# Eight-by-eight max pool subtracted from its own input: five buffers of five rows, smaller first pieces and a longer jump

## Chip, core, metric

One core of one Trainium2 chip. The metric is device time in microseconds (us) of the whole program, here of one core. The verdict for a change is faster, same or slower at a limit of 2%.

## The reference

```python
def reference(x):                       # x: 8 x 64 x 256 x 256, float32
    x_r = x.reshape(B, C, oH, 8, oW, 8)
    pooled = x_r.max(axis=(3, 5))
    upsampled = np.repeat(np.repeat(pooled, 8, axis=2), 8, axis=3)
    return (x - upsampled).astype(np.float32)
```

A "row" below is eight image lines, 2048 floats or 8 KB. Each of the 128 partitions holds whole rows and gets 128 of them: 134.22 MB come in, as many go out.

## The kernel before

```python
HEAD = [[2, 2]]      # the first tile, in pieces of so many rows
SIZE = 4             # rows of a whole tile
ROUNDS = 5           # turns of the vector engine's loop
TAIL = [2, 1, 1]     # the last tile, stored in pieces
SLOTS = 6            # buffers
SKIP = 52            # instructions that a jump passes
# ... (layout and semaphores cut)
    def pool_and_subtract(slot, lo, R, wait):
        # ...
        if wait is not None:
            take(wait, 16)                    # wait for the load
        nc.vector.tensor_reduce(...)          # max of each 8 x 8 window, R rows
        take(reduced, 1)
        for r in range(R):
            sub = nc.vector.tensor_tensor(...)  # in place, a row each
        sub.then_inc(ready, 1)
# ... SyncE: a load per piece; waits for stored[slot] before a buffer is loaded again
# ... ScalarE: a store per piece, after ready; at the end it waits for the last stores
        with nc.vector.If_eq(turns, 0):       # never taken: turns is ROUNDS
            for _ in range(SKIP):
                nc.vector.sem_inc(skipped, 1)
        # ... head pieces
        with nc.vector.Fori(0, ROUNDS):
            for j in range(SLOTS):
                slot = (HEADS + j) % SLOTS
                pool_and_subtract(slot, 0, SIZE, loaded[slot])
        # ... tail pieces
```

Three streams run side by side: loads, the vector engine, stores (vector engine and data queues are busy for 90% and 99.6% of the span, below). The guarded instructions never run (the page counts 364 instructions with a jump of 52 and, in jump_only, of 72); they move the loop to another place in the vector engine's instruction stream.

## Time and profile before

| | before |
|---|---|
| timed, median | 627.71 us |
| span of the profiled execution | 626.0 us |
| vector engine busy | 562.6 us (90%) |
| the two data queues, share of 16 DMA engines | 99.6% |

The page and its views are shown in the prediction. It is the last microseconds in slices of one microsecond; the columns are the slice, its length, busy time of the vector engine and of GpSimd, the TensorE clock, the mean busy share of the 16 DMA engines, and their rate in GB/s:

```profile
622.00:623.00 1.00, 0.00 (x0) 0.00 (x0) 1.00 0.95 401
623.00:624.00 1.00, 0.00 (x0) 0.00 (x0) 1.00 0.55 229
624.00:625.00 1.00, 0.00 (x0) 0.00 (x0) 1.00 0.02 8
```

A share of 0.06 is one DMA engine of sixteen (1/16). After 624 us one engine alone is still at work, for a part of the slice.

### The profile page before, as it was taken

What the parts mean: (1) busy time and instruction counts of PE and PEld (TensorE: products, weight loads), DVE (VectorE), ACT (ScalarE), POOL (GpSimd) and SP (SyncE); (2) the same over time, 40 slices, a digit from 0 to 9 for tenths busy, and PEclk for the clock granted to TensorE, in tenths of its full rate; (3) what the DMA queues carried; (4) which work ended last, traced back from release to release, by engine and by line L of the source; (5) the groups of instructions that cost most, each with busy time, mean ns of one, the idle gap of its engine ahead of it and who ended that gap; (6) DMA issues with size and microseconds to landing.
All of it is one profiled execution on the core that took longest, in us unless ns stands there. A gap on an engine that the chain in (4) does not pass through costs nothing. (4 is left out here: it accounts for less than half of the span.)

```text
span 626.0 us, 364 instructions
## 1 busy us (share of the span) xinstructions
DVE 562.6 (90%) x163; POOL 0.2 (0%) x4
## 2 busy tenths in 40 slices
DVE  4999999998998888988889888898888998888983
POOL 0000000000000000000000000000000000000000
DMA  8999999999999999999999999999999999999998
GB/s 369 399 436 437 436 436 436 436 433 427 429 431 436 427 431 436 436 436 436 436 436 436 436 431 429 427 433 429 431 433 436 436 436 436 436 436 436 436 429 343
DMA packets 9793, 268.45 MB, mean 429 GB/s; under 512 B 1088, under 2 KB 1088, under 8 KB 1088
## 3 DMA queue, kind: packets, MB, share of 16 engines
q1 hardware_dynamic: 4752, 134.22, 49.9%
q10 hardware_dynamic: 5040, 134.22, 49.7%
q14 instruction: 1, 0.01, 0.0%
HBM read 134.22 MB, written 134.22 MB: 429 GB/s over the span
## 5 line engine op out<-in xcount | busy, mean ns | idle before, releaser
L73 DVE TENSOR_REDUCE tops<-dat 128x128 f32<-128x8192 f32 (+2 forms) x35 | 278.3, 7953 | 48.9 <-DVEq L65 48.9
L85 DVE TENSOR_TENSOR dat<-dat,tops 128x2048 f32<-128x2048 f32 x128 | 285.0, 2286 | 5.2
L157 POOL MEMSET const-bfloat16-1.0<- 128x1 bf16 x1 | 0.1, 101 | 0.0
L157 POOL MEMSET const-uint8-127<- 128x1 uint8 x1 | 0.1, 101 | 0.0
L157 POOL MEMSET const-float32-0.0<- 128x1 f32 x1 | 0.1, 98 | 0.2 <-issue 0.2
L157 POOL MEMSET const-float32-1.0<- 128x1 f32 x1 | 0.1, 98 | 0.0
## 6 DMA issues: line engine op xcount, KB each, us to landing
dat<-in_x_dram SPq DMA_DIRECT2D x31, 4096.0 KB, 62.5
out_dram<-dat ACTq DMA_DIRECT2D x30, 4096.0 KB, 35.8
out_dram<-dat ACTq DMA_DIRECT2D x3, 2048.0 KB, 19.6
dat<-in_x_dram SPq DMA_DIRECT2D x2, 2048.0 KB, 9.6
out_dram<-dat ACTq DMA_DIRECT2D x2, 1024.0 KB, 9.3
```

The lines of the kernel that those rows point to most:

```text
L73: nc.vector.tensor_reduce(out=maxs if R > 1 else maxs[:, 0], in_=(wins.rearrange("p r ph ow pw -> p r ow ph pw") if R > 1 else wins[:, 0]. ...
L85: sub = nc.vector.tensor_tensor(out=wins[:, r], in0=wins[:, r], in1=maxs[:, r].unsqueeze(1).unsqueeze(3).to_broadcast([P, pH, oW, pW]), op ...
L157: nc = _bacc.Bacc("TRN2", target_bir_lowering=False, num_devices=1)
```

## The change

Fewer and larger transfers (tiles of five rows in five buffers), a head of small pieces so that the first result can be stored sooner, and a longer jump, meant to spare the loop a fetch of instructions in each turn.

```diff
-HEAD = [[2, 2]]
-SIZE = 4
-ROUNDS = 5
+HEAD = [[1, 1, 2], [2, 3], [5], [5], [5]]
+SIZE = 5
+ROUNDS = 4
 TAIL = [2, 1, 1]
-SLOTS = 6
-SKIP = 52
+SLOTS = 5
+SKIP = 72
@@
-                pool_and_subtract(i, lo, R, first[k])
+                pool_and_subtract(i % SLOTS, lo, R, first[k])
```

## The prediction

The sum in it is 0.36 us saved, from 627.71 to about 627.35. All of it comes from the steady transfers, per DMA engine 0.29 us for 64 packets fewer and 0.07 us for 8 completion writes fewer; every other part is put at 0. In rival (a), "a sixth of the bandwidth" is an estimate from the bytes of the two queues from 26 to 50 us, 7.18 against 3.41 MB with packets of 32 against 16 KB.

> **What bounds the kernel now.** I read first the page's busy shares, slices and waits, then the sums by stretch, then the transfers in order of time at both ends. The page:
>
> ```profile
> span 626.0 us, 364 instructions
> DVE 562.6 (90%) x163; POOL 0.2 (0%) x4
> GB/s 369 399 436 437 436 436 436 436 433 427 429 431 436 427 431 436 436 436 436 436 436 436 436 431 429 427 433 429 431 433 436 436 436 436 436 436 436 436 429 343
> q1 hardware_dynamic: 4752, 134.22, 49.9%
> q10 hardware_dynamic: 5040, 134.22, 49.7%
> q14 instruction: 1, 0.01, 0.0%
> ```
>
> The vector engine is 90% busy, but the two data queues together hold the 16 DMA engines for 99.6% of the span. Only the first two slices and the last fall well below 436 GB/s; the dips to 427 in the middle are whole packets falling into one slice or the next. The sums by stretch:
>
> ```profile
> 2.00:4.00 2.00, 0.00 (x0) 0.00 (x0) 1.00 0.88 295
> 18.00:26.00 8.00, 7.85 (x3) 0.00 (x0) 1.00 0.95 356
> 26.00:100.00 74.00, 73.41 (x22) 0.00 (x0) 1.00 1.01 436
> 100.00:580.00 480.00, 437.44 (x126) 0.00 (x0) 1.00 1.00 433
> 620.00:624.00 4.00, 0.00 (x0) 0.00 (x0) 1.00 0.89 375
> ```
>
> The last number is the rate. 433 holds both while the vector engine has no pause (26 to 100 us) and while it pauses before each tile (100 to 580 us), so its speed does not set the rate. Waits from 150 to 580 us:
>
> ```profile
> DVE tops L73 <- DVEq L65: 37.5, 23, 1.6
> ```
>
> It waits 1.6 us for each tile's load. And the end, in order of time:
>
> ```profile
> 598.35 4.42 DVE L73 TENSOR_REDUCE tops<-dat 128x64 f32<-128x4096 f32 x1 [1.64 <-DVEq L65]
> 614.39 2.29 DVE L85 TENSOR_TENSOR dat<-dat,tops 128x2048 f32<-128x2048 f32 x1
> ```
>
> The last subtract ends at 616.7 us, but that 1 MB store lands at 624.9: older stores were still queued. The end is bound by transfers too, and a vector engine that finished sooner would gain nothing.
>
> [...] from 26 to 50 us, while the loads run in 32 KB packets and the first stores in 16 KB ones, the queues moved 7.18 and 3.41 MB, 2 to 1; later, with 32 KB on both sides, 104.11 and 103.84. [...] The trace's instruction packets are 8 KB[...], and one falls in the span.
>
> **The change part by part.** Work is the same 128 rows of 8 KB per partition, each moved in and out.
>
> Steady transfers. A packet of 8, 16 or 32 KB occupies a DMA engine 309, 611 or 1213 ns, that is 301 ns per 8 KB and 9 ns more; successive packets start about 4 ns before the last has ended, so a packet really costs about 4.5 ns beyond its bytes at 27.2 GB/s (435.2 GB/s for 16). Check: a 4-row tile is 8 packets in and 8 out per DMA engine, 16 x (1204.7 + 4.5) ns, and two completion writes of 9 ns: 19.37 us; loads land every 19.36 us (114.15, 133.52, 152.88). With 5 rows: 16 x (1505.9 + 4.5) ns + 18 ns = 24.18 us, or 4.837 us a row against 4.841. Counted over the kernel: before 33 loads and 35 stores, 68 x 8 = 544 packets per DMA engine; after 29 loads (eight head pieces, 20, 1) and 31 stores (8, 20, 3), 480. Saved: 64 x 4.5 ns = 0.29 us and 8 x 9 ns = 0.07 us, 0.36 us together.
>
> Vector work. A reduce takes 2279, 4417, 8685 ns for 1, 2, 4 rows: 2135 per row and 144 fixed, so 6.55 us for 3 and 10.82 us for 5. Before 30 x 8.685 + 3 x 4.417 + 2 x 2.279 = 278.4 us; after 23 x 10.82 + 6.55 + 3 x 4.417 + 4 x 2.279 = 277.8 us. The 128 subtracts (2.205 us start to start) stay. A 5-row tile takes 10.82 + 5 x 2.205 + 0.13 = 22.0 us, under the 24.18 us of its transfers. 0.6 us less busy, on an engine that has slack: worth 0.
>
> Head. The first piece of one row should land about 2.4 us sooner (5.9 us in place of 8.3), and the first store be issued at about 10.6 in place of 17.5. But the DMA engines are already full of loads by then (441 GB/s from 4 to 18 us), and the same 24 rows of loads are issued at once in both kernels. Starting sooner moves bytes from load time to store time; it removes none. Worth 0, save for the one-time bubble where the first store joins the loads: 18 to 26 us at 356 GB/s loses about 1 us beside the plateau. It should move to about 13 us and stay about as long.
>
> Tail. Same pieces, same last store, and again stores are queued behind each other: worth 0.
>
> Slots. 25 rows of buffer in place of 24 (203 KB per partition by shapes in place of 195). A buffer's round of load, compute and store before is 62.5 + 17.9 + 35.8 = 116.2 us = 6 x 19.36. After it must be 5 x 24.18 = 120.9 us, of which compute 22; so 99 us of transfers, 4.1 tile transfers waiting or moving at any time. The DMA engines run dry only if both queues empty together[...].
>
> Jump. [...] Worth 0 as long as no fetch recurs each turn; even then a turn has 5 x 2.2 = 11 us of slack.
>
> Sum: 0.36 us saved, from 627.71 to about 627.35.
>
> **The rivals.** (a) Small store packets are starved. An 8 KB store packet against a 40 KB load packet gets a sixth of the bandwidth, so tile 0's stores drag. I followed it by hand: 8 rounds of row 0 against 16 and 24 KB loads end at about 22.6 us, 8 of row 1 at 34, 8 of two rows against 40 KB (2.125 us a round) at 51; slot 0 is free then, as before (its next load was issued at 51.7). Tile 1 frees at about 88 us, when some 3 rows of loads are still queued: close, but not dry, and the store backlog would take all the bandwidth anyway. So worth 0 in time; what it does is leave a deeper store queue and a shallower load queue than before. If both did run dry for some us: 628 to 632. (b) The vector engine becomes the bound, by a fetch each turn or by slots that come free late: against it stand 22.0 against 24.18 us per tile and the deep store queue; it needs over 10 us a turn lost. Then 630 to 645. (c) The earlier start counts in full because the early vector engine is never idle (the slices read 9 from the second on): then 2 to 5 us less, 623 to 625. The 8 us of queued stores behind the last subtract speak against it. (d) 40 KB packets run less well than 32 KB [...]: the 8, 16 and 32 KB sizes all lie on one straight line, which speaks against it; 1% worse would be 633.
>
> **Range and chances.** The three runs before differ by 0.35 us. The bubble and the ragged end may each move by some tenths. I predict 627.3, with 626.5 to 628.3 to hold 8 times in 10, a bit more room above for (a). Faster by 2% would mean under 615.2 us, and 268.44 MB at 435.2 GB/s take 616.8 alone: 0.005. Slower by over 2% needs (b) or (d) badly: 0.015. Within 2%: 0.98.
>
> **What would show it.** Right: both queues with 99% or more of the span; 40 KB packets and 4176 and 4464 packets on the two queues; loads landing 24.2 us apart; DVE busy about 562 us, 5-row reduces of 10.82 us, a wait of about 2.1 us before each in the second half; first store issued near 10.6 us and yet the same end; loads taking less time to land than 62.5 us and stores more than 35.8. Wrong: a slice in the middle well under 430 GB/s, an idle vector engine between 30 and 100 us, more than a few instruction packets, or a last store that lands 3 us after its issue (then the vector engine bounds the tail).

## The result

629.01 us in the median of six runs (628.81 to 629.48) against 627.71 (627.41 to 627.85): ratio 1.0023, 95% interval 1.0010 to 1.0036. By the limit of 2% that is "same", but it is a real 1.3 us the wrong way, and outside the predicted 626.5 to 628.3. A ratio here is the mean time of one kernel's fast runs over that of the other's of the same rounds, so not quite the ratio of the medians. All of these runs are fast.

The page of the changed kernel:

```profile
span 627.0 us, 342 instructions
DVE 561.3 (90%) x159; POOL 0.2 (0%) x4
q1 hardware_dynamic: 4176, 134.22, 49.8%
q10 hardware_dynamic: 4464, 134.22, 49.6%
q14 instruction: 1, 0.01, 0.0%
dat<-in_x_dram SPq DMA_DIRECT2D x23, 5120.0 KB, 41.7
out_dram<-dat ACTq DMA_DIRECT2D x23, 5120.0 KB, 57.0
```

The packet counts, the busy time of the vector engine and the shallower load queue (41.7 us from issue to landing) beside a deeper store queue (57.0) are as predicted. The sums by stretch:

```profile
12.00:18.00 6.00, 5.85 (x3) 0.00 (x0) 1.00 0.98 385
18.00:40.00 22.00, 21.71 (x7) 0.00 (x0) 1.00 1.01 433
40.00:46.00 6.00, 5.85 (x4) 0.00 (x0) 1.00 1.03 414
100.00:580.00 480.00, 442.40 (x122) 0.00 (x0) 1.00 1.00 433
580.00:620.00 40.00, 27.10 (x12) 0.00 (x0) 1.00 1.00 431
```

The plateau is the same 433 GB/s, and nothing runs dry. The bubble where stores join the loads has come in two halves, at 12 to 18 and at 40 to 46 us. The waits from 150 to 580 us:

```profile
DVE tops L73 <- DVEq L65: 34.5, 16, 2.7
```

That is 2.2 us before each tile, as predicted. The vector engine's end:

```profile
589.22 4.41 DVE L73 TENSOR_REDUCE tops<-dat 128x64 f32<-128x4096 f32 x1
605.25 2.29 DVE L85 TENSOR_TENSOR dat<-dat,tops 128x2048 f32<-128x2048 f32 x1
```

The last subtract ends at 607.5 us, 9.2 us sooner than before (616.7), and it gains nothing. Now the last slices, to be laid beside those of before:

```profile
622.00:623.00 1.00, 0.00 (x0) 0.00 (x0) 1.00 0.89 377
623.00:624.00 1.00, 0.00 (x0) 0.00 (x0) 1.00 0.10 41
624.00:625.00 1.00, 0.00 (x0) 0.00 (x0) 1.00 0.06 25
625.00:626.00 1.00, 0.00 (x0) 0.00 (x0) 1.00 0.02 8
```

Here the loss is. From 623 to 624 the share is 0.10 where it was 0.55: nearly all DMA engines have finished half a microsecond sooner than before. But from 624 to 625 it is 0.06, exactly one engine, busy all the time, and it goes on to 625.5.

The trace has a record for each packet with its start and duration, and a completion write of 4 bytes for each DMA engine at the end of each transfer. The 16 completion writes of the very last store tell how far apart the engines are (ns from the median engine, which stands first in us; worked out from these records):

```
before   median 623.63 us:  -209 -197 -182 -172 -171  -89  -19   -8    8   41   73   74  136  143  164   942
changed  median 623.05 us:  -164 -135 -116 -112  -39  -31  -25   -1    1   26   97  108  114  123  515  2454
```

In the changed kernel the median engine ends 0.58 us sooner than in before, but one engine is 2.45 us behind it where the late one of before was 0.94 behind. The load queue's 4176 packets are 29 loads of 144, eight data packets and a completion write for each of 16 engines. This fits with no engine taking over another's packets, and an engine that is late stays late: in the run before_long_jump below, the last completion writes of loads and stores alike stay 1.46 to 1.47 us behind the median from 50 us to the end. The kernel ends with its slowest engine.

The ledger of the two profiled executions (629.17 and 627.78 us, 1.39 apart): the median engine ends 0.58 sooner; the slowest is 1.51 further behind it; from its last packet to the span's end, 0.04 more; and the time outside the span (timed less span) is 2.20 against 1.78, 0.42 more. The sum is 1.39.

Where does the late engine lose its time? One packet in the span belongs to queue q14, which the trace calls an instruction packet: that it brings a part of the vector engine's program is read from the runs below, where its time moves with the jump (4.1 us with a jump of 72, 12.3 with 52). The records don't name the DMA engine of a packet; packets are followed by their times, as one starts about 4 ns before the last one of its engine ends. Packets at 4 us in the changed kernel and at 17 us in before, from the records:

```
            start ns  duration  queue         bytes
changed         4144       311  instruction    8192
                4451       841  load           8192   (309 is usual)
before         17261       309  instruction    8192
               17566      1795  load          32768   (1213 is usual)
```

The one instruction packet occupies an engine for 0.31 us and the load packet after it is stretched by 0.53 or 0.58 us: 0.84 and 0.89 us in all. In before that is nearly the whole lateness of 0.94. In the changed kernel it is 0.84 of 2.45 (the first load's completion writes already show one engine 838 ns late); 0.4 us more come by 19 us, while the stores join. The rest: six load packets after 50 us are stretched by more than 25 ns (in before, none), four of them, at 160.44, 209.26, 233.62 and 257.86 us, by 430, 164, 52 and 591 ns. The late engine's completion writes of the loads jump by 0.42, 0.17, 0.06 and 0.60 us at just these tiles. They lie one or two tile periods (24.18 us) apart, each within 0.4 us of the end of a store on the median engine (160.75, 209.14, 233.33, 257.54 us).

### The profile page after: what moved, and what is told of

It reads as the page before. It is cut to its first block, busy times and chain, and to the rows that moved or that the text cites. A ratio compares the mean times of both kernels' runs of the same rounds, so it can differ in the third digit from the quotient of the medians.

```text
span 627.0 us, 342 instructions
## 1 busy us (share of the span) xinstructions
DVE 561.3 (90%) x159; POOL 0.2 (0%) x4
## 3 DMA queue, kind: packets, MB, share of 16 engines
q1 hardware_dynamic: 4176, 134.22, 49.8%
## 5 line engine op out<-in xcount | busy, mean ns | idle before, releaser
L73 DVE TENSOR_REDUCE tops<-dat 128x160 f32<-128x10240 f32 (+3 forms) x31 | 277.7, 8958 | 41.7 <-DVEq L65 41.7
## 6 DMA issues: line engine op xcount, KB each, us to landing
dat<-in_x_dram SPq DMA_DIRECT2D x23, 5120.0 KB, 41.7
```

Source lines behind the costliest of these rows:

```text
L73: nc.vector.tensor_reduce(out=maxs if R > 1 else maxs[:, 0], in_=(wins.rearrange("p r ph ow pw -> p r ow ph pw") if R > 1 else wins[:, 0]. ...
```

## The experiments

The theory after the first look: the end is set by the slowest DMA engine; an instruction packet makes one engine late, and something else makes it later. "Late" below means behind the median engine. The rivals for that something: the longer jump by itself, the small head pieces, or five rows (40 KB packets, shallow load queue).

For each run the trace gave: the time of its instruction packet; the lateness of the slowest engine at the last store; the number of load and store packets between 50 and 600 us stretched by more than 25 ns; and the **gap**: on the median engine, the time from the end of a load to the end of the next store, in turns of one load and one store packet (2.42 us with 32 KB, 3.02 with 40 KB). That an engine takes them in turn is read from the records: in before from 100 to 580 us, a packet and the next of its engine are of different queues in all 2416 cases in which their times leave only one choice. The gap stays the same to within 0.1 turn from about 100 to 560 us, but for two runs that have a range in the table. It came to matter in the second round.

| run | timed median, lowest to highest | ratio to before | timed less span | instruction packet at us | gap | slowest late by us | stretched |
|---|---|---|---|---|---|---|---|
| before | 627.71, 627.41–627.85 | 1 | 1.78 | 17.3 | 6.9 | 0.94 | 0 |
| changed kernel | 629.01, 628.81–629.48 | 1.0023 | 2.17 | 4.1 | 3.0 | 2.45 | 6 |
| jump_only | 627.82, 627.71–630.33 | 1.0006 | 1.83 | 4.8 | 7.0 | 3.65 | 45 |
| head_only | 642.81, 642.21–644.31 | 1.0240 | 1.78 | 18.3 | 1.0–1.4 | 4.16 | 617 |
| five_rows_old_head | 628.78, 627.25–629.62 | 1.0010 | 2.25 | 4.7 | 6.0 | 2.69 | 15 |
| after_short_jump | 626.65, 626.42–626.77 | 0.9979 | 1.77 | 12.3 | 2.0 | 0.59 | 3 |
| before_delayed | 630.30, 629.63–633.11 | 1.0054 | 1.81 | 19.6 | 0.0–0.2 | 3.24 | 114 |
| head_only_delayed | 627.28, 626.87–627.79 | 0.9993 | 1.80 | 19.9 | 3.0 | 1.00 | 3 |
| short_jump_delayed | 626.72, 626.49–626.91 | 0.9985 | 1.79 | 12.9 | 4.0 | 0.30 | 2 |
| after_delayed | 627.41, 627.30–628.20 | 0.9998 | 2.23 | 4.1 | 5.0 | 1.24 | 2 |
| short_jump_gap3 | 626.65, 626.49–628.90 | 0.9995 | 1.79 | 12.3 | 3.0 | 0.30 | 0 |
| after_gap4 | 627.97, 627.44–632.99 | 1.0020 | 2.22 | 4.1 | 4.5 | 0.92 | 0 |
| before_later_fetch | 627.61, 627.34–627.77 | 0.9998 | 1.74 | 26.8 | 6.6 | 0.79 | 0 |
| before_long_jump | 630.07, 628.15–632.62 | 1.0049 | 2.02 | 4.5 | 7.0 | 1.46 | 0 |
| after_jump60 | 628.84, 628.64–628.94 | 1.0016 | 1.74 | 4.0 | 3.0 | 2.71 | 17 |

The columns from "timed less span" on are of the one profiled execution, with its span rounded to 0.1 us. All runs in the table are fast by the 1.5% rule, those near 633 us too. Before, run beside them, gave medians of 627.65 to 627.69.

### Round one: one part of the change at a time

**jump_only.**

```diff
-SKIP = 52
+SKIP = 72
```

> Before with nothing changed but the jump (72 in place of 52). Straggler theory (one DMA engine, held up by an 8 KB instruction packet, ends last; the rest of its lateness in the changed kernel comes from elsewhere): one instruction packet in the span, moved from 17 us to about 4, one DMA engine about 0.85 us behind the median at the end, time within 0.2 us of before (627.7). Rival, the jump itself costs the 1.3 us (by its early instruction packet): 628.7 to 629.3, lateness over 2 us.

Four of six runs gave 627.71 to 627.83, as the theory has it; two gave 630.05 and 630.33, and the profile fell on the latter: three engines over 3.5 us late, with store packets stretched from 58 to 95 us. The jump alone does not cost the steady 1.3 us; but the early instruction packet seems to make such single bad runs likelier. Before itself had one run of 629.07 among eleven in this round, so the kernel is not free of them.

**head_only.**

```diff
-HEAD = [[2, 2]]
+HEAD = [[1, 1, 2]]
-SKIP = 52
+SKIP = 49
```

> Before with the head's first tile cut into 1, 1, 2 rows, jump shortened by three so that the loop stands at the same instruction. Straggler theory: 627.6 to 627.9, one DMA engine about 0.9 us late, no stretched packets after 60 us. Rival, the small head pieces unsettle the DMA engines: 628.5 to 629.3, with stretched packets and lateness over 1.5 us.

Both expectations fell: 642.81 us, ratio 1.0240 (1.0227 to 1.0254), fifteen microseconds for one more head piece. The trace shows the DMA engines busy all the time and slow. From 130.5 to 134.5 us:

```profile
130.50:134.50 4.00, 4.00 (x2) 0.00 (x0) 1.00 1.06 377
100.00:580.00 480.00, 427.88 (x122) 0.00 (x0) 1.00 1.00 423
```

The first line is one burst, 377 GB/s; the second says that the plateau as a whole is at 423 in place of 433. The stretched load packets (525, three in four of them by 100 to over 1000 ns) come in bursts once a tile, where the engines pass from one store to the next, and only here is a load's end just one turn ahead of it. That gave the gap as a suspect.

**five_rows_old_head.**

```diff
-HEAD = [[1, 1, 2], [2, 3], [5], [5], [5]]
+HEAD = [[2, 2], [5], [5], [5], [5]]
-SKIP = 72
+SKIP = 78
```

> The changed kernel with the old head pieces of 2 and 2 rows and then four whole tiles of five (jump set so that the loop stands where it does in the changed kernel). If the small pieces cause the lateness: 627.0 to 627.4, since the median DMA engine should end near 623.1 us and the late one 0.9 later. If five slots or 40 KB packets cause it: 628.6 to 629.5, with stretched load packets after 60 us.

Scattered, 627.25 to 629.62, a median of 628.78. Neither expectation covers the scatter. The small pieces are not what makes the changed kernel slow: without them an early packet (4.7 us) and a late engine (2.69) are still there. And at a gap of six, 15 packets are stretched all the same. The load packets at 80.77 and 105.30 us are so by 334 and 391 ns, and at the completion of just these two loads the slowest engine has fallen behind by 414 ns more each time.

**after_short_jump.**

```diff
-SKIP = 72
+SKIP = 52
```

> The changed kernel with the old jump of 52. If the jump's place of the fetch causes the lateness: about 627.3, or more instruction packets and a time of 630 or more if [...] each turn fetches (each packet about 0.85 us on some DMA engine[...]). If the jump is not the cause and no turn fetches: 629.0 as the changed kernel.

626.65 us (626.42 to 626.77), ratio to before 0.9979, interval 0.9966 to 0.9992. Twenty instructions fewer in the jump turn the changed kernel's loss into a gain, and the time is below either expectation. The loop does not fetch in each turn: there is one instruction packet in the span, at 12.3 us. Its last slices:

```profile
622.00:623.00 1.00, 0.00 (x0) 0.00 (x0) 1.00 0.80 336
623.00:624.00 1.00, 0.00 (x0) 0.00 (x0) 1.00 0.04 16
624.00:625.00 1.00, 0.00 (x0) 0.00 (x0) 1.00 0.00 0
```

Nobody works after 624 us. The median engine ends at 622.94 us, as in the changed kernel (623.05), and the slowest 0.59 later. But two things changed at once: the packet came at another time, and as the first piece landed sooner (all engines by 5.08 us in place of 5.90) the first store came sooner and the gap is two instead of three. Round two separates them.

### Round two: moving the gap

A reduce with no use, ahead of the first real one, delays the first store and so shifts stores against loads (see the gaps in the table); everything else stays. The edit (with the jump one shorter, so that the loop keeps its place):

```diff
+                if k == 0:
+                    take(first[0], 16)
+                    nc.vector.tensor_reduce(out=idle[:, :], in_=dats[0][:, :DELAY],
+                                            axis=mybir.AxisListType.X, op=mybir.AluOpType.max)
-                pool_and_subtract(i, lo, R, first[k])
+                pool_and_subtract(i, lo, R, first[k] if k else None)
```

**before_delayed** (before, DELAY = 2048).

> Before with one idle reduce of one row (2.28 us) ahead of the first real one, so that the first store joins the loads two 32 KB load packets later. Boundary theory (what stretches load packets is how many packets lie between the end of one load and the end of the next store on a DMA engine; bad at one, as in the kernel with only the head changed): the gap goes from seven packets to one, and the time to 638 to 645 with hundreds of stretched packets. Rival, small pieces or early stores in themselves did it: 627.5 to 628.5, no stretched packets.

Right in direction, wrong in size: the gap came out at 0.2 or less, not 1, and the time at 630.30 (1.0054) with 114 stretched packets, not at 640. The delay of 2.28 us costs 2.6 us against before. The median engine ends as it did (623.56 us against 623.64); the slowest is 3.24 late.

**head_only_delayed** (head_only, DELAY = 2048).

> The kernel with only the head changed (642.8) and the same idle reduce of 2.28 us. Boundary theory: the gap goes from one packet to three, and the time falls to 627.5 to 629.5. Rival, small pieces in themselves: it stays at 641 to 645.

As the boundary theory had it, and below its range: 627.28 us in place of 642.81, from 2.3 us of useless work. The same stretch is back at full rate:

```profile
130.50:134.50 4.00, 4.00 (x2) 0.00 (x0) 1.00 1.08 467
100.00:580.00 480.00, 442.30 (x126) 0.00 (x0) 1.00 1.00 433
```

(467 in four microseconds is whole packets counted at their start.) So it is not the small pieces by themselves: the 15 us go away when the stores are shifted against the loads, from a gap of 1.0 to 1.4 turns to one of 3.0.

**short_jump_delayed** (changed kernel, SKIP = 51, DELAY = 680).

> The changed kernel with the old jump (626.65) and an idle reduce of 680 columns, 0.85 us, which is what the early instruction packet cost the changed kernel at its first landing. If the changed kernel is slow through the later first store (gap of three packets in place of two): 628.5 to 629.5 with a late DMA engine of over 2 us. If through the lateness that the early instruction packet gives to one DMA engine: 626.5 to 627.2, late engine under 1 us.

626.72, the slowest engine 0.30 late. A later first store does not slow the kernel; but the gap came out at four, not three, so it did not yet test three.

**after_delayed** (changed kernel, SKIP = 71, DELAY = 680).

> The changed kernel itself with the same idle reduce of 0.85 us: the early instruction packet stays, the gap goes to four or five packets. If the gap of three is what stretches the late engine's loads: 627.3 to 628.0 (late engine about 0.9 to 1.3 us behind). If the early packet is: 628.6 to 629.6.

627.41: the changed kernel with 0.85 us of useless work put in is 1.6 us faster. The early packet is still there (4.1 us) and the slowest engine is 1.24 us late, about half of 2.45. So half of the lateness went when the gap changed, and half was left, with the early packet still there.

### Round three: packet and gap crossed

**short_jump_gap3** (changed kernel, SKIP = 51, DELAY = 290).

> The changed kernel with the old jump (instruction packet near 12 us instead of 4) and an idle reduce of 290 columns (0.45 us), meant to set the changed kernel's own gap of three packets. If it takes both, the early packet and the gap of three: 626.4 to 627.2, slowest DMA engine under 0.8 us late. If the gap of three alone stretches loads: 628 to 629.5, over 2 us late.

Gap 3.0 as meant, no stretched packet, the slowest engine 0.30 late; four runs of six at 626.49 to 626.65, two at 628.5 and 628.9 that no profile caught, and that lie in the range of "the gap of three alone". Its last slices:

```profile
622.00:623.00 1.00, 0.00 (x0) 0.00 (x0) 1.00 0.87 369
623.00:624.00 1.00, 0.00 (x0) 0.00 (x0) 1.00 0.02 8
```

**after_gap4** (changed kernel, SKIP = 71, DELAY = 290).

> The changed kernel (early instruction packet) with the idle reduce of 0.45 us, for a gap of four. If it takes both: 627.2 to 627.9, the slowest DMA engine 0.85 to 1.3 us late from the packet at 4 us alone. If the early packet alone costs it all: 628.8 to 629.5, over 2 us late.

Gap 4.5, slowest engine 0.92 late, no stretched packet. Three runs at 627.44 to 627.54, as "it takes both" has it; the others at 628.39, 628.73 and 632.99. The scatter leaves the ratio unclear against before (0.9996 to 1.0045).

Crossed: in each field the lateness of the slowest engine in the profiled executions, the range of all runs, and in how many runs the slowest engine ended over 1.5 us late. For runs without a profile the lateness is an estimate: that of the profiled execution plus the difference of the two spans, as if the median engine ended at the same time.

| | packet near 12 us | packet near 4 us |
|---|---|---|
| gap 3 | 0.30 us; 626.49 to 628.90; 2 of 6 | 2.45 and 2.71 us (changed kernel; after_jump60, below); 628.64 to 629.48; 11 of 11 |
| gap 2, 4 or 5 | 0.59 and 0.30 us; 626.42 to 626.91; 0 of 10 | 0.92 and 1.24 us; 627.30 to 632.99; 4 of 11 |
| gap 6 or 7 (five_rows_old_head, jump_only; before_long_jump, below) | not run | 2.69, 3.65 and 1.46 us; 627.25 to 632.62; 8 of 16 |

Before, with its packet at 17 us and a gap of 6.9, was over 1.5 us late in 2 of the 40 runs beside the experiments. So the early packet makes one engine late at every gap, by 0.9 to 1.5 us in the profiled executions in which no packet was stretched after 50 us. With a gap of three it was over 2 us late in every run. But a gap of three is not the only way to it: at the other gaps, too, 12 of 27 runs with an early packet ended over 1.5 us late, and 2 of 6 with a gap of three and a packet at 12 us. What the gap of three adds is that the loss comes each time.

**before_later_fetch.**

```diff
-SKIP = 52
+SKIP = 49
```

> Before with a jump of 49, so that the instruction packet comes after the stores have joined (near 26 us instead of 17). If what counts is that the packet holds up one DMA engine wherever it falls: 0.85 to 1.0 us late, 627.5 to 627.8. If it holds it up less while loads and stores are mixed (only its own 0.31 us): 0.4 to 0.6 late, 627.1 to 627.4.

627.61 and 0.79 us late, with the packet at 26.8 us amid loads and stores: between the two expectations and nearer the first. A packet there goes with about as much lateness. The small lateness of 0.30 to 0.59 us belongs to packets at 12 to 13 us, just where the stores join and load packets are stretched on nearly all engines anyway (in the changed kernel, whose first store packet starts at 15.0 us, 15 load packets that start from 14.20 to 14.53 us take 738 to 973 ns in place of 611); that the two overlap is argued from the times, not shown.

**after_far_jump.**

```diff
-SKIP = 72
+SKIP = 200
```

> The changed kernel with a jump over 200 instructions[...]. Instruction-packet theory: two or more packets in the first 10 us, each 0.85 us for one DMA engine: two late engines, or one 1.7 us or more behind; 629 to 631 at a gap of three packets, 628 to 629 at another gap. If instruction packets don't matter: as the gap that comes out has it, 626.5 to 627.5 at a gap other than three.

Two packets, at 2.1 and 7.3 us. Three of seven runs were slow (681 to 692 us), and the profile fell on one of them, so its lateness is not used; the fast ones lie from 627.88 to 632.57, ratio 1.0046. Inconclusive, but a warning.

### Round four: the 0.42 us outside the span

Timed less span is 2.14 to 2.25 us in every run of the kernels of five rows with a jump of 71 or more, and 1.73 to 1.83 in all others up to here.

**before_long_jump.**

```diff
-SKIP = 52
+SKIP = 112
```

> Before with a jump over 112 instructions: its vector program is then as long as the changed kernel's (112 + 10 + 44 + 11 = 177 against 72 + 48 + 42 + 11 = 173). If length makes the time outside the span: timed less span about 2.2 us in place of 1.78. If five rows or their early packet make it: 1.75 to 1.85. Either way an instruction packet near 4 or 5 us and one DMA engine at least 0.85 us late.

1.92 to 2.15 us outside the span in its four runs, with four rows: above the 1.83 of the shorter programs, though under the expected 2.2. So it goes with the length of the jump, and not with five rows; as jump_only, with 72 but four rows, has 1.83, it seems to be the length of the whole program that counts. And the trace has a second 8 KB instruction packet, at 628.0 us, after the span's end (626.2); that this packet is what costs the time is not shown. (In the changed kernel's trace no record reaches so far.) Two runs of 628.2 and two of 632 show the scatter of early packets again.

**after_jump60.**

```diff
-SKIP = 72
+SKIP = 60
```

> The changed kernel with a jump over 60: twelve instructions shorter (161), [...] the packet stays near 4 us and the gap at three packets. If both causes are right: timed less span 1.8 us, slowest DMA engine still over 2 us late, 628.4 to 629.1. If the outside part goes with the early packet: timed less span 2.2 and 628.8 to 629.5. If the packet does not come early: about 626.7.

All as expected: 1.74 to 1.79 outside the span, the packet at 4.0 us, a gap of 3.0, 628.84 us. And the lateness is there again, 2.71 us, with load packets stretched at 160.29, 184.91, 209.39 and 233.90 us by 433, 286, 331 and 565 ns, nearly the moments of the changed kernel. Its last slices look like the changed kernel's:

```profile
623.00:624.00 1.00, 0.00 (x0) 0.00 (x0) 1.00 0.08 33
624.00:625.00 1.00, 0.00 (x0) 0.00 (x0) 1.00 0.06 25
625.00:626.00 1.00, 0.00 (x0) 0.00 (x0) 1.00 0.04 16
```

## Why the prediction was wrong

**Right.** That transfers set the time, and that a faster vector engine gains nothing: its last work ended 9.2 us sooner for no gain. The count of packets and their cost: loads land 24.18 us apart, and the median engine gained 0.58 us in place of the 0.36 predicted (summed over the packet records, the changed kernel was ahead by 0.12 us of bytes at 100 us and by 0.43 at 580). The reduces (10.82 us for five rows: 23 took 248.8), the waits, the queues' depths, the bubble (it came in two halves that sum to about as much). The first store came at 11.27 us and not at 10.6, because the late engine held back the first landing (after_short_jump, without it: 10.33).

**Wrong, first: "The bubble and the ragged end may each move by some tenths."** The prediction reckoned for the mean of 16 engines and took the spread of their ends as noise. It was a term of its own: the slowest engine went from 0.94 to 2.45 us behind the median, 1.51 us, more than all that the larger packets saved. Before's lateness stood in its own trace, with the instruction packet that made it, and was read past as a "ragged end".

**Wrong, second: "Jump ... Worth 0 as long as no fetch recurs each turn".** No fetch recurred: one instruction packet is in the span. But the jump's length decides when that packet comes and how long the program is. By the runs, its twenty instructions cost 0.42 us outside the span (gone with a jump of 60), and move the packet from 12 to 4 us, where it makes one engine 0.84 us late at once. With the gap of three turns that lateness grew to over 2 us in every run, 2.45 in the profiled one. The padding was not needed either: with a jump of 52 no fetch recurred (one packet, at 12.3 us). Set back to 52, the same five rows give 626.65 us, below the 627.3 predicted.

**The rivals.** The time fell into the range of rival (a), 628 to 632, but its mechanism did not happen: neither queue ran dry and the rate from 18 to 40 us was 433 GB/s. Rivals (b) to (d) did not happen either.

**Open.** Why the engine that the early packet made late has further packets stretched, each time with a gap of three and in part of the runs with other gaps, and why a gap of zero or one turn stretches a hundred packets and more, is not settled: the runs show that it depends on the gap, not what collides. The single bad runs of up to five microseconds stay unexplained as well; before has them too (629.07 and 628.64 among the 40).

## What to carry to other kernels

When transfers bound a kernel and each transfer is split evenly over the DMA engines, read the end of the slowest engine, not the mean rate: one instruction packet cost its engine 0.84 us here, more than the 0.36 us that 64 packets fewer were reckoned to save. Treat the place of a program's code, its length, and the spacing between the ends of loads and of stores as settings to try: twenty unused instructions were worth 2.4 us here, and 2.3 us of useless work won back 15. Compare such versions over several runs, because a layout can be good in the median and have a bad run in three (short_jump_gap3: 628.5 and 628.9 us among six).
